# Output projection of a hybrid attention layer: where its weights and outputs wait, which engine adds, and the order of the first up tile's products

## Chip, core, metric

The kernel runs on one core of a Trainium2 chip. The metric is device time in microseconds (us) of one execution. A core has TensorE (PE, matrix products and transposes), VectorE (DVE), ScalarE (ACT), GpSimd (POOL) and SyncE (SP), which here only issues transfers. Each engine works through its own queue in order and waits on semaphores for the others.

## What is computed

One layer over 1024 positions with 1024 features, float32 in and out: two attention head groups, an output projection with a gated residual, then a gated MLP with a causal convolution of width 3.

```python
mixed = jnp.dot(jnp.concatenate([o_mla, o_ca], axis=-1), w_out[l])
x = x + g_a[:, None, :] * mixed

h = modulate(rmsnorm(x, g_mlp_norm[l]), sh_m, sc_m)
u = causal_dwconv(jnp.dot(h, w_up[l]), conv_w[l], conv_b[l])
gate, val = jnp.split(u, 2, axis=-1)
x = x + g_m[:, None, :] * jnp.dot(jax.nn.silu(gate) * val, w_down[l])
```

## The kernel before

Every product is made of three TensorE matmuls on split operands: a high part (a rounded copy, made by `hi_of`) and a low part (the rest, made by `lo_of`); `hi*hi + hi*lo + lo*hi` is summed in PSUM (`gemm3`, `product`). A split is thus one copy on ScalarE and one subtract on GpSimd or VectorE, for each operand tile.

The stages, in the order of the program:

1. Input projections, then attention. Attention handles units (a head and one half of the queries), four row tiles of 128 each. For each row tile the probabilities are split into two 16-bit parts and transposed by a transfer from SP's queue (line 822); `values` multiplies them with v, and after four tiles a unit's output is scaled and written to DRAM, `oT_d` (lines 853 to 859). Input projections of later heads, the up-projections `f_up` and the chunk-attention half of the output projection, `f_oca`, are filled in between. `f_oca` multiplies rows 512 to 1023 of `w_out` and writes the partial sums to DRAM, `part_d`.
2. The output projection's other half (lines 989 to 1055): `load_wo` fetches eight weight pieces of 128x512 through staging tiles and splits them into pages of the pool G4 (8 buffers). Then, for each of eight row tiles t: load the attention output `ol` (256 KB) and split it, load x and the partial sum `pa` (512 KB each), 24 matmuls into PSUM `op`, then three sums, `pa + op`, times the gate `gabc`, plus x; store the result (`x1_d`), take its square sum (ScalarE) and reciprocal root (GpSimd), and scale it in place to `xn2[t]`.
3. Operand pages for the MLP. `mod_T(k, h)` transposes block k of half h (0: tiles 0 to 3, 1: tiles 4 to 7) and applies scale and shift; `bpage` splits. The up projection uses a seven-product scheme of Strassen type in 2x2 blocks: pages b11 and b21 come from half 0, and t3, t1, b22, t2 and t4 are differences of halves, made on VectorE block by block, k = 0 to 3 (lines 1116 to 1127).
4. 22 up tiles, `ff_tile(j)`. `ff_load(j)` fetches two weight tiles `wu` of 512 KB and splits wa and wb; `ff_sums(j)` forms five sums and splits them (wc to wg); `product(..., "t3")` and so on multiply, 12 matmuls each; sums into `c`, convolution, SiLU, product, store.
5. The down projection and the final residual.

The program is written in this order, but a scheduler, working on its own estimates, arranges each engine's queue: a step can be moved ahead of others where its inputs allow, and `tc.issue_after` forces an order. A tile pool with n buffers for a tag lets an instruction that needs a new buffer wait until the oldest one's readers are done; a pool opened in the place of a closed one waits for the tiles that lay there.

Names of buffers in the profile are shortened: `wor` is a staged piece of w_out, `wo` its split page, `ol` and `oh` the attention output's low and high part, `om` a unit's output on its way to `oT_d`, `x`/`x_d` the residual stream and its store, `hv` and `t`/`b` values and pages of stage 3, `p` the PSUM tiles and copies of the up tiles, `PTm`/`hlm` the transposed probabilities and their two parts.

Of the kernel before, what the change touches and what calls it, by code (L numbers as in the profile page):

```python
# [63 lines left out]
def layer_kernel(ctx, tc, I, out):  # L64
# [661 lines left out]
    class Unit:  # L726
# [7 lines left out]
        def scores(u, i):  # L734
# [55 lines left out]
            with tc.high_priority(offset=OFF_P):  # L790
                dve.reciprocal(ri[:], rsum[:, 0:1])
                dve.tensor_scalar(ri[:], ri[:], PSCALE, None, op0=MUL)  # L792
                for x, (p0, p1) in enumerate(pieces):
# [28 lines left out]
                    anchor["sp"] = sp.dma_start_transpose(tt[:, b0:b0 + 2 * w // P, :], hl[:, :2 * w]).ins  # L822
# [4 lines left out]
        def values(u, i):  # L827
# [17 lines left out]
            with tc.high_priority(offset=OFF_V):  # L845
# [7 lines left out]
                if i % 4 == 3:  # L853
                    dst = at.tile([P, 512], F32, name=f"o{u.nm}_{u.g}", tag="o", bufs=1)
# [4 lines left out]
                    sp.dma_start(u.dst_d[r0, u.g * 512:(u.g + 1) * 512], dst[r0])  # L859
# [3 lines left out]
    pair = [0]  # L863
    biases = {}
# [124 lines left out]
    wo = [load_wo(0, n, "a", "v" if n else "p") for n in range(2)]  # L989
    att.__exit__(None, None, None)  # L990
    att_pg.__exit__(None, None, None)
    psA.__exit__(None, None, None)
    G["cm3"].__exit__(None, None, None)
    G["cmv"].__exit__(None, None, None)
# [13 lines left out]
    def mod_T(k, h):  # L1008
# [3 lines left out]
        v = tb.tile([P, 512], F32, name=f"hv2_{k}_{h}", tag="v", bufs=11)  # L1012
# [12 lines left out]
    sp.dma_start(cvp[:], I["pack"][:, C_CV:])  # L1025
    gabc = gb.tile([P, D], F32, name="gabc")
    sp.dma_start(gabc[:], ga_d[:])
    for t in range(NT):
        lo = gb.tile([P, 4, P], F32R, name=f"ol{t}", tag="ol", bufs=3)
        hi = gb.tile([P, 4, P], F32R, name=f"oh{t}", tag="oh", bufs=3)  # L1030
        sp.dma_start(f32(lo[:]), oT_d[0:4, :, t * P:(t + 1) * P].rearrange("k p t -> p k t"))
        hi_of("a", hi[:], f32(lo[:]))
        lo_of("p", lo[:], f32(lo[:]), hi[:])
        x1 = tb.tile([P, D], F32, name=f"x1_{t}", tag="x1", bufs=8)
        sp.dma_start(x1[:], I["x"][t * P:(t + 1) * P, :])
        pa = gb.tile([P, D], F32, name=f"pa{t}", tag="pa", bufs=3)
        sp.dma_start(pa[:], part_d[t])
        pt = ps2.tile([P, 1024], F32, name=f"op{t}", tag="op", bufs=3)
        for n in range(2):
            gemm3(pt[:, n * 512:(n + 1) * 512],  # L1040
                  [(hi[:, k], lo[:, k], wo[n][k][:, 0], wo[n][k][:, 1]) for k in range(4)])
        dve.tensor_tensor(pa[:], pa[:], pt[:], op=ADD)
        dve.tensor_tensor(pa[:], pa[:], gabc[:], op=MUL)
# [6 lines left out]
        if t % 4 == 3:  # L1050
            h = t // 4
            if h == 0:
                for k in range(ND):
                    v0[k] = mod_T(k, 0)
                    bpage("b11" if k < 4 else "b21", k % 4, v0[k], "v" if k % 2 else "p")
# [454 lines left out]
```

## Time and profile before

| | |
|---|---|
| median of three runs | 1411.35 us (1406.68 to 1412.14) |
| the profiled execution | 1412.2 us, its span 1410.4 us |
| TensorE busy | 1237.9 us (88%), mean granted clock 0.928 |
| VectorE busy | 1099.7 us (78%) |
| GpSimd busy | 712.9 us (51%) |
| ScalarE busy | 620.9 us (44%) |
| moved by transfers | 190.57 MB, mean 135 GB/s |

The profile records one execution. Times count from the start of the span. "Busy" sums the durations of an engine's instructions; TensorE's matmuls overlap their neighbours, so a single matmul's duration is longer than the distance to the next. The granted clock is the share of TensorE's full clock that the throttle let through. A row of the timeline names the instruction, what it writes and reads, and in brackets how long its engine sat idle before it and on whom it waited. The prediction shows the lines on which it rests.

### The profile page before, as it was taken

What the parts mean: (1) busy time and instruction counts of PE and PEld (TensorE: products, weight loads), DVE (VectorE), ACT (ScalarE), POOL (GpSimd) and SP (SyncE); (2) the same over time, 40 slices, a digit from 0 to 9 for tenths busy, and PEclk for the clock granted to TensorE, in tenths of its full rate; (3) what the DMA queues carried; (4) which work ended last, traced back from release to release, by engine and by line L of the source; (5) the groups of instructions that cost most, each with busy time, mean ns of one, the idle gap of its engine ahead of it and who ended that gap; (6) DMA issues with size and microseconds to landing.
All of it is one profiled execution on the core that took longest, in us unless ns stands there. A gap on an engine that the chain in (4) does not pass through costs nothing.

```text
span 1410.4 us, 18704 instructions
## 1 busy us (share of the span) xinstructions
PE 1237.9 (88%) x6156; PEld 1012.0 (72%) x6156; DVE 1099.7 (78%) x1861; ACT 620.9 (44%) x1129; POOL 712.9 (51%) x685
## 2 busy tenths in 40 slices
PE   4889798998777689886686999999999999999998
PEld 3788487887656467674565887777778777888886
DVE  6957778675689988873577888988888888788667
ACT  4343445444556545543264444344334443443331
POOL 5454556375555754334563677676667875200000
PEclk9999797999787899996887999999999999999999
DMA  8314558664322667677721323333222223894451
GB/s 313 126 37 83 137 145 185 152 138 106 70 48 46 133 144 170 144 147 222 278 98 45 105 98 127 127 112 128 97 100 87 101 101 117 306 354 128 127 163 60
DMA packets 223689, 190.57 MB, mean 135 GB/s; under 512 B 148708, under 2 KB 166884, under 8 KB 223592
## 3 DMA queue, kind: packets, MB, share of 16 engines
q1 hardware_dynamic: 223592, 189.38, 47.4%
q8 instruction: 48, 0.79, 0.2%
q14 instruction: 49, 0.40, 0.1%
HBM read 117.24 MB, written 37.49 MB: 110 GB/s over the span
## 4 chain that ended last, share of the span: by engine, by line
DVE 21%; PE 17%; POOL 6%; issue 6%; ACT 4%; DMA 2%; SPq 0%; DVEq 0%; POOLq 0%; ACTq 0%
DVE u L1174 5%; DVE u L1173 4%; PE dnA_P L1321 2%; PE dnA_P L1322 2%; PE dnA_P L1323 2%; ACT u L1172 2%; PE dnB_P L1322 1%; PE dnB_P L1321 1%; PE dnB_P L1323 1%; DVE u L1250 1%; DVE c L1245 1%; DVE gmbc L1160 1%; DVE wu L1102 1%; DVE wu L1101 1%; DVE ws L1099 1%
## 5 line engine op out<-in xcount | busy, mean ns | idle before, releaser
L76 ACT ACTIVATE dnP<-dnr 128x1024 fp32r<-128x1024 f32 x73 | 77.3, 1061 | 110.9 <-PE dnA_P L1323 46.4
L1295 DVE TENSOR_TENSOR dnP<-dnr,dnP 128x1024 fp32r<-128x1024 f32 x72 | 90.7, 1264 | 44.4 <-ACT dnP L76 44.2
L1173 DVE SCALAR_TENSOR_TENSOR u<-c,cvp,u 128x1023 f32<-128x1023 f32 x44 | 82.6, 1917 | 47.2 <-ACT u L1172 45.6
L72 POOL TENSOR_SCALAR hlm<-Pm,rim 128x512 f16<-128x512 f32 (+3 forms) x96 | 68.7, 724 | 85.2 <-DVE rim L792 21.6
L1174 DVE SCALAR_TENSOR_TENSOR u<-c,cvp,u 128x1022 f32<-128x1022 f32 x44 | 86.4, 2003 | 0.0
L72 POOL TENSOR_SCALAR hlc<-Pc,ric 128x640 f16<-128x640 f32 (+2 forms) x64 | 46.7, 732 | 72.8 <-DVE ric L792 46.4
L811 DVE SCALAR_TENSOR_TENSOR hlm<-Pm,rim,hlm 128x512 f16<-128x512 f32 (+3 forms) x96 | 67.7, 715 | 8.6 <-POOL hlm L72 8.1
L850 PE MATMUL pvm<-PTm,vt 128*128 128x256 f16 (+1 forms) x320 | 47.0, 295 | 30.3 <-DMA PTm<-hlm 29.7
L789 ACT ACTIVATE Pm<-sm,mm 128x128 f32<-128x128 f32 (+3 forms) x64 | 47.3, 739 | 55.6 <-DVE mm L782 37.5
L850 PEld LDWEIGHTS <-vt 128*128 128x128 f16 x320 | 31.2, 108 | 46.8 <-issue 22.2
L789 ACT ACTIVATE Pc<-sc,mc 128x640 f32<-128x640 f32 (+2 forms) x64 | 42.1, 658 | 46.6 <-DVE mc L778 35.4
L811 DVE SCALAR_TENSOR_TENSOR hlc<-Pc,ric,hlc 128x640 f16<-128x640 f32 (+2 forms) x64 | 50.7, 795 | 14.1 <-POOL hlc L72 13.3
L76 ACT ACTIVATE wc<-ws 128x512 fp32r<-128x512 f32 x22 | 13.9, 633 | 103.0 <-DVE ws L1099 103.0
L1172 ACT ACTIVATE u<-c,cvp 128x1024 f32<-128x1024 f32 x44 | 52.1, 1234 | 14.8 <-DVE c L1245 7.8
L153 PE MATMUL ipq<-wq_s,hT 128*128 128x256 f32 x192 | 57.4, 301 | 1.2 <-ACT wq_s L76 1.2
L154 PE MATMUL ipq<-wq_s,hT 128*128 128x256 f32 x192 | 57.7, 301 | 0.1
L155 PE MATMUL ipq<-wq_s,hT 128*128 128x256 f32 x192 | 57.3, 299 | 0.0
L1249 ACT ACTIVATE u<-u 128x1024 f32<-128x1024 f32 x22 | 23.3, 1061 | 71.1 <-DVE u L1174 71.0
L83 POOL TENSOR_TENSOR wc<-ws,wc 128x512 fp32r<-128x512 f32 x22 | 34.3, 1557 | 36.4 <-ACT wc L76 36.4
L1322 PE MATMUL dnA_P<-dnP 128*128 128x512 f32 x132 | 51.3, 389 | 0.0
L1323 PE MATMUL dnA_P<-dnP 128*128 128x512 f32 x132 | 51.3, 389 | 0.0
L1321 PE MATMUL dnA_P<-dnP 128*128 128x512 f32 x132 | 51.2, 389 | 0.0
(420 smaller groups left out, 4563.0 us busy)
## 6 DMA issues: line engine op xcount, KB each, us to landing
wu<-w_up SPq DMA_DIRECT2D x44, 512.0 KB, 3.5
dnr<-g_d SPq DMA_DIRECT2D x73, 256.0 KB, 4.5
aw<-w_ada SPq DMA_DIRECT2D x48, 256.0 KB, 3.6
g_d<-u SPq DMA_DIRECT2D x22, 512.0 KB, 2.7
dnr<-w_down SPq DMA_DIRECT2D x44, 256.0 KB, 5.4
adaw<-w_ada_a SPq DMA_DIRECT2D x16, 512.0 KB, 6.5
x<-x SPq DMA_DIRECT2D x16, 512.0 KB, 8.7
g_d<-gs SPq DMA_DIRECT2D x22, 256.0 KB, 2.0
```

Source lines behind the costliest of these rows:

```text
L72: pool.tensor_scalar(o, i, s, 1.0, op0=MUL, op1=MUL)
L76: act.activation(o, i, AF.Copy)
L789: act.activation(pr[:, :n], sv, AF.Exp, bias=m[:], scale=-1.0, accum_out=rsum[:, 0:1])
L811: dve.scalar_tensor_tensor(hl[:, w:2 * w], pp, ri[:], hl[:, :w], op0=MUL, op1=SUB)
L850: last = pe.matmul(dst, u.vst(j), mov, start=(x == 0), stop=(x == len(todo) - 1), skip_group_check=True)
L1172: act.activation(u[:], c, AF.Identity, scale=cvp[:, cv + 2:cv + 3], bias=cvp[:, cv + 3:cv + 4])
L1173: dve.scalar_tensor_tensor(u[:, 1:], c[:, :S - 1], cvp[:, cv + 1:cv + 2], u[:, 1:], op0=MUL, op1=ADD)
L1174: dve.scalar_tensor_tensor(u[:, 2:], c[:, :S - 2], cvp[:, cv:cv + 1], u[:, 2:], op0=MUL, op1=ADD)
L1295: r = f(*a, **k)
L1321: pe.matmul(pt, sh, w[:, 0, 0], start=start, stop=False, skip_group_check=add)
L1322: pe.matmul(pt, sh, w[:, 1, 0], start=False, stop=False, skip_group_check=add)
L1323: pe.matmul(pt, sl, w[:, 0, 0], start=False, stop=stop, skip_group_check=add)
```

## The change

The parts, with the names of the diff:

- `load_wo` stages w_out in `atile` (tag A, five buffers, used until then by the adaLN weights) in place of `qtile` (two buffers, shared with attention's squares and copies). This holds for both halves of w_out.
- The last unit's output goes to a `qtile` instead of the single `o` buffer. Its store to `oT_d` is held back and issued behind the first four `ol` loads; the last row tile's transposes are ordered behind the store of the unit before.
- A pool `go` holds `ol` and `oh`, four buffers each instead of three, in the place of the q and k tiles of attention; `o_load` for tiles 0 to 3 stands ahead of the loop, and tile t+4 is loaded after tile t's products. `pa` has four buffers and, with x, is loaded by `x_load`, four tiles ahead too.
- All sums and scalings of stage 2 are on VectorE (some were on GpSimd).
- `ff_load(0)` is issued among the loads, and `ff_sums(0)` after tile 1's sums; the pages `ws` move to a pool that is opened earlier.
- The transposes of half 0 come after tile 4 rather than after tile 3.
- Pages t3 and t2 take the eight buffers of G4, the pool of w_out's pages, instead of new ones.
- Tile 0's five products of stage 3's pages are computed block by block inside the loop that makes the pages, into PSUM of the old stage (`p34`, `p56`, `p7`); its sums into `c0` follow directly. `ff_tile(0)` skips those products and sums.

```diff
     def load_wo(k0, n, he, le):
...
-            raw = qtile(f"wor{k}_{n}")
+            raw = atile(f"wor{k}_{n}")
...
-                        anchor["sp"] = sp.dma_start_transpose(tt[:, b0:b0 + 2 * w // P, :], hl[:, :2 * w]).ins
+                    with tc.issue_after(anchor["om"]) if u is units[-1] and i == 7 else contextlib.nullcontext():
+                        anchor["sp"] = sp.dma_start_transpose(tt[:, b0:b0 + 2 * w // P, :], hl[:, :2 * w]).ins
...
-                    dst = at.tile([P, 512], F32, name=f"o{u.nm}_{u.g}", tag="o", bufs=1)
+                    final = u is units[-1]
+                    dst = qtile(f"o{u.nm}_{u.g}") if final else \
+                        at.tile([P, 512], F32, name=f"o{u.nm}_{u.g}", tag="o", bufs=1)
...
-                    sp.dma_start(u.dst_d[r0, u.g * 512:(u.g + 1) * 512], dst[r0])
+                    if final:
+                        held.append(lambda: sp.dma_start(u.dst_d[r0, u.g * 512:(u.g + 1) * 512], dst[r0]))
+                    else:
+                        anchor["om"] = sp.dma_start(u.dst_d[r0, u.g * 512:(u.g + 1) * 512], dst[r0]).ins
...
+    mlp0 = tc.tile_pool(name="mlp0", bufs=1, side="right", reuse_waits="tile")
+    mp = {"a": mlp0.__enter__()}
+    goo = tc.tile_pool(name="go", bufs=1, side="right", reuse_waits="tile")
+    go = goo.__enter__()
+    def o_load(t):
+        ol[t] = go.tile([P, 4, P], F32R, name=f"ol{t}", tag="ol", bufs=4)
+        oh[t] = go.tile([P, 4, P], F32R, name=f"oh{t}", tag="oh", bufs=4)
+        anchor["ol"] = sp.dma_start(f32(ol[t][:]), oT_d[0:4, :, t * P:(t + 1) * P].rearrange("k p t -> p k t")).ins
+        hi_of("a", oh[t][:], f32(ol[t][:]))
+        lo_of("p", ol[t][:], f32(ol[t][:]), oh[t][:])
+
+    for t in range(4):
+        o_load(t)
+    with tc.issue_after(anchor["ol"]):
+        held[0]()
...
+    sp.dma_start(gabc[:], ga_d[:])
+    for t in range(2):
+        x_load(t)
+    raw0, wa0, wb0 = ff_load(0)
+    for t in range(2, 4):
+        x_load(t)
+    sp.dma_start(cvp[:], I["pack"][:, C_CV:])
     for t in range(NT):
-        lo = gb.tile([P, 4, P], F32R, name=f"ol{t}", tag="ol", bufs=3)
-        hi = gb.tile([P, 4, P], F32R, name=f"oh{t}", tag="oh", bufs=3)
...
+        if t + 4 < NT:
+            o_load(t + 4)
...
-        (dve if t % 2 or t > 5 else pool).tensor_tensor(x1[:], x1[:], pa[:], op=ADD)
+        dve.tensor_tensor(x1[:], x1[:], pa[:], op=ADD)
         sp.dma_start(x1_d[t], x1[:])
         act.activation(pa[:], x1[:], AF.Square, accum_out=ss2[:, t:t + 1])
+        if t + 4 < NT:
+            x_load(t + 4)
...
-        (dve if t > 5 else pool).tensor_scalar(x1[:], x1[:], r2[:, t:t + 1], 1.0, op0=MUL, op1=MUL)
-        if t % 4 == 3:
+        dve.tensor_scalar(x1[:], x1[:], r2[:, t:t + 1], 1.0, op0=MUL, op1=MUL)
+        if t == 1:
+            w0 = ff_sums(0, raw0)
+        if t == 4:
...
+    ready = p34[:], p56[:, :512], p56[:, 512:], p7[:, :512]
     for k in range(4):
...
         bpage("t3", k, t3, "v")
+        product(ready[3], w0[0], "t3", ks=[k])
...
         bpage("t1", k, b12, "v")
+        product(ready[1], w0[2], "t1", ks=[k])
         bpage("b22", k, b22, "v")
+        product(ready[0][:, :512], w0[4], "b22", ks=[k])
...
         bpage("t2", k, b22, "v")
+        product(ready[2], w0[1], "t2", ks=[k])
...
         bpage("t4", k, v0[k + 4], "v")
+        last = product(ready[0][:, 512:], w0[3], "t4", ks=[k])
...
+    dve.tensor_tensor(c0[:, 0], pc[:, :512], pc[:, 512:], op=ADD)
+    dve.tensor_tensor(c0[:, 1], pc[:, :512], ready[2], op=ADD)
+    dve.tensor_tensor(c0[:, 2], c0[:, 1], ready[3], op=ADD)
+    dve.tensor_tensor(c0[:, 1::2], c0[:, 1:3], ready[1].unsqueeze(1).to_broadcast([P, 2, 512]), op=ADD)
+    dve.tensor_tensor(c0[:, 1:3], c0[:, 1:3], ready[0].rearrange("p (a b) -> p a b", a=2), op=ADD)
```

More of the change, by code (lines that the diff above doesn't have):

```diff
@@ L1269, in layer_kernel @@
     gr_gen = gate_row()
[L1270 to L1271 removed]
+    p3_last = [last]
+    cur = w0 + [None, None, c0]
     for j in range(NF):
```

120 lines of the change are left out of this document (60 added, 60 removed).

## The prediction

> **What bounds the kernel now.** I began with the first line of the profile's page, for the execution's own time, and then asked how busy each engine is in stretches cut at the places where the program changes stage. The time around the span is 1412.2 - 1410.4 = 1.8 us, and I make the sum against 1412.2 us, 0.85 us above the median of the three runs (1411.35 us).
>
> ```profile
> span 1410.4 us, 18704 instructions
> ```
> The table by stretches follows; its columns are the stretch, its length, the busy time of TensorE (PE), its weight loads (PEld), VectorE (DVE), ScalarE (ACT) and GpSimd (POOL) with their instructions, the granted TensorE clock, the DMA share and GB/s. The first row lies inside attention, the second is its end, the next three hold the output projection, then come the operand pages (732 to 758), up tile 0's own products (758 to 775) and the other 21 up tiles.
>
> ```profile
> 472.00:503.00 31.00, 18.22 (x91) 13.45 (x89) 27.52 (x71) 15.09 (x31) 26.48 (x23) 0.78 0.76 154
> 640.00:657.00 17.00, 6.15 (x29) 3.89 (x29) 5.47 (x9) 3.90 (x7) 5.45 (x7) 0.50 0.79 190
> 657.00:676.00 19.00, 18.87 (x69) 14.89 (x70) 3.17 (x4) 5.45 (x9) 7.56 (x6) 0.83 0.67 229
> 676.00:690.00 14.00, 2.99 (x9) 1.57 (x7) 10.17 (x7) 5.01 (x9) 7.69 (x4) 0.67 1.04 382
> 690.00:732.00 42.00, 39.35 (x180) 31.62 (x181) 23.14 (x20) 17.55 (x30) 30.82 (x31) 0.95 0.48 178
> 732.00:758.00 26.00, 10.33 (x38) 7.47 (x36) 25.07 (x38) 18.75 (x32) 3.03 (x2) 0.63 0.00 0
> 758.00:775.00 17.00, 16.12 (x63) 12.73 (x64) 9.28 (x11) 5.78 (x11) 11.17 (x8) 0.87 0.29 93
> 775.00:1173.00 398.00, 386.69 (x1668) 312.18 (x1667) 344.82 (x275) 163.29 (x237) 282.67 (x177) 1.00 0.32 108
> ```
> The last row settles how a microsecond counts: the up tiles keep TensorE busy 386.69 of 398 us at clock 1.00, so they are bound by TensorE, and work that reaches them earlier ends earlier by the same amount. From 657 to 775 TensorE is busy only 18.87 + 2.99 + 39.35 + 10.33 + 16.12 = 87.7 of 118 us. The holes are 11 us at 676 to 690 and 15.7 us at 732 to 758. In the second VectorE is busy 25.07 of 26 us, so VectorE bounds that stage and TensorE's work is queued behind it. The first hole is read from the queue on SyncE and from TensorE's own timeline (start, length, engine, line, operation; in brackets the idle time before it and what ended it).
>
> ```profile
> 645.00 0.58 SPq L859 DMA_DIRECT2D oT_d<-om  x1
> ...
> 650.04 0.38 SPq L1031 DMA_DIRECT2D ol<-oT_d  x1
> ...
> 660.98 9.78 SPq L661 DMA_DIRECT2D wor<-w_out  x3
> 670.81 0.42 SPq L1025 DMA_DIRECT2D cvp<-pack  x1
> 674.45 2.25 SPq L1035 DMA_DIRECT2D x<-x  x5
> 676.75 3.14 SPq L1031 DMA_DIRECT2D ol<-oT_d  x3
> ```
> ```profile
> 656.90 0.80 PE L153 MATMUL op<-wo,oh 128*128 128x512 f32 x1 [4.44 <-ACT oh L76]
> ...
> 685.76 0.79 PE L153 MATMUL op<-wo,oh 128*128 128x512 f32 x1 [8.84 <-ACT oh L76]
> ```
> The three last weight loads hold the in-order queue from 660.98 to 670.76, because their two staging buffers are not free; the loads of x (674.45) and of the attention output for tiles 3 to 5 (676.75) stand behind them. TensorE runs out of tiles and waits 8.84 us for tile 3's high part. The end of each stage stands on VectorE's timeline.
>
> ```profile
> 720.64 1.22 DVE L1042 TENSOR_TENSOR pa<-pa,op 128x1024 f32<-128x1024 f32 x1 [1.08 <-PE op L155]
> ...
> 729.77 0.89 DVE L1049 TENSOR_SCALAR x<-x,r 128x1024 f32<-128x1024 f32 x1 [2.38 <-DMA x_d<-x]
> ...
> 732.56 0.69 DVE L1119 TENSOR_TENSOR t<-hv,hv 128x512 f32<-128x512 f32 x1 [1.30 <-ACT hv L1013]
> ...
> 755.64 1.47 DVE L83 TENSOR_TENSOR t<-hv,t 128x512 fp32r<-128x512 f32 x2
> ...
> 775.18 1.22 DVE L1245 TENSOR_TENSOR c<-c,p 128x1024 f32<-128x1024 f32 x1
> ```
> The last projection product ends just before 720.64; the pages run from 732.56 to 755.64 + 1.47 = 757.1; up tile 0's last sum, which waits for its last product, starts at 775.18.
>
> **The change part by part.**
>
> *Start of the projection.* The staging tiles for w_out move from two shared buffers to five free ones, so in the changed order thirteen of sixteen loads stand inside attention and the last three directly behind its last transposes, ahead of the attention-output loads. What is not moved is the dependence: tile 0 needs the output rows written by the transfer issued at 645.00, and its loads stay behind the last transposes, at about 650 as now. On ScalarE tile 0's high part now stands behind the last attention copies and one weight split. I take a start at 656.3 instead of 656.90: a gain of 0.6 us, with bounds of 0 and, if the loads went out right behind the 645.00 write, 5.
>
> *The projection itself.* Eight tiles of 24 matmuls are 192. The chain of waits shows what one costs, second column, at the two clock rates:
>
> ```profile
> 659.05 0.43 PE op L153
> ...
> 664.65 0.23 PE op L153
> ```
> 192 x 0.23 = 44.2 us, which rounded up also carries the eight short transposes that stand among them. After attention's idle end the clock is low: 0.83 granted over 19 us with half rate at first means 19 x 0.17 x 2 = 6.5 us at half rate, which costs 3.2 us. The Trainium skill, in "TensorE: Matmul & The Clock Gate" (Part 1: The HAM clock gate), gives about 3.4 us of sustained work before full rate; by that page the surcharge would be an estimated 1.7 us and the gain of the whole 1.5 us more; this trace does not agree, so the row decides. With 1.5 us of waits for the first low parts the last product ends at 656.3 + 44.2 + 3.2 + 1.5 = 705.2 in place of 720.6: 15.4 us with the start included.
>
> This needs inputs in time. Per tile VectorE now has all four sums:
>
> ```profile
> L1042 DVE TENSOR_TENSOR pa<-pa,op x8: 1215/1222/1224, 676.0 to 720.6; 128x1024 f32<-128x1024 f32 x8
> L1043 DVE TENSOR_TENSOR pa<-pa,gabc x8: 1217/1368/3364, 679.5 to 723.4; 128x1024 f32<-128x1024 f32 x8
> L1046 ACT ACTIVATE pa<-x x8: 1051/1057/1064, 684.0 to 726.8; 128x1024 f32<-128x1024 f32 x8
> L1046 ACT ACTIVATION_READ_ACCUMULATOR pa<-x x8: 184/187/194, 685.0 to 727.8; 128x1 f32 x8
> L1044 DVE TENSOR_TENSOR x<-x,pa x5: 1214/1226/2178, 685.0 to 724.6; 128x1024 f32<-128x1024 f32 x5
> L1044 POOL TENSOR_TENSOR x<-x,pa x3: 2404/3025/3290, 681.0 to 706.7; 128x1024 f32<-128x1024 f32 x3
> ```
> 1.22 + 1.37 + 1.23 and the scale, 0.89 in the row at 729.77, are 4.7 us against 24 x 0.23 = 5.5 us of TensorE: VectorE stays just below. Leaving GpSimd takes 2.4 to 3.3 us of add per tile off its queue, in front of the low-part splits that TensorE waits for. The x loads no longer stand behind the weights; I expect them to be issued near 660 instead of 674.45. Each tile's square on ScalarE (1.06 us) and its mean now stand ahead of the split of the tile four later, on both queues; with x landed by about 668 that split is ready when TensorE comes to it, with x as late as now TensorE waits 674.45 - 660 = 14.5 us less the two tiles (11 us) of lead, so 3.5, and two delayed splits make it 6. Bounds of this part: -2 to +6 around my value. The bytes are not the bound: eight tiles with x, partial sum and store of 0.52 MB each and 0.26 MB of outputs, and 1 MB of up weights, are some 16 MB, in 55 us 290 GB/s; the row at 676 moved 382. Tile 0's seven weight splits on GpSimd lie in that stretch as well, where it was busy 7.56 of 19 us; they cost nothing while it has room, and about 1.3 us each if they delay an output split.
>
> *From the last product to the first page.* 11.9 us now (720.64 to 732.56), a chain of sums, the store of x that must finish before x is scaled in place, transposes and copies. The last x add was one of those lengthened by GpSimd (up to 2178 ns against 1214); that goes: 1.0 us gained, bounds 0 and 2.
>
> *The pages.* The same VectorE instructions in the same number (x38 in their row): 24.5 us as now. The products of tile 0 go between them, five after each block, 60 matmuls of 0.23 = 13.8 us, into a stage where TensorE is busy 10.33 of 26: covered by VectorE's 25 us. If the cover is gone (half rate), 60 x 0.43 = 25.8 us and 10.33 make 36.1, which is 10 us too much. Transposes of blocks 2 and 3 now stand behind waits for earlier blocks' pages on TensorE's in-order queue, with ScalarE's copies and VectorE's differences behind them; there is slack of a block, and I add nothing here, bounds 0 and +10.
>
> *After the pages.* Now 757.1 to 775.18, 18.1 us, for splits of tile 0's weights, 60 products and the wait for the second weight load of tile 1. In the changed order two sums come first (2 x 24.5/38 = 1.3 us), which free the bank of tile 1's first product; this product, done within the pages until now, then takes 12 x 0.23 = 2.8 us. From there both kernels do the same. 18.1 - 4.1 = 14.0 us gained, less 1 us that I allow for tile 1's first splits: 13.0; bounds 10 and 14.
>
> *Attention.* The splits of the first w_out half move out of 472 to 503, where GpSimd was busy 26.48 of 31 us and VectorE 27.52, five of the eight to a place ahead of the second head group's up-projections; five of the second half's go into the last heads. One split costs this:
>
> ```profile
> L76 ACT ACTIVATE wo<-wor x16: 620/630/633, 475.2 to 673.1; 128x512 fp32r<-128x512 f32 x16
> L83 POOL TENSOR_TENSOR wo<-wor,wo x12: 1260/1298/3231, 476.6 to 658.2; 128x512 fp32r<-128x512 f32 x12
> ```
> Eight of them are 8 x 1.30 = 10.4 us of GpSimd; if all of it had been on the path, that would be the gain; moved work can as well delay the place where it lands. I take 0, bounds -10 and +10.
>
> **The sum.** 15.4 + 1.0 + 0 + 13.0 + 0 = 29.4 us. 1412.2 - 29.4 = 1382.8, predicted 1383 us. Its own range is 1376 to 1391.
>
> **The rivals.**
>
> *TensorE becomes the bound of the pages.* For: all rows at 732 to 758 show a clock of 0.63, and short bursts with gaps are what the new order makes. Against: the row at 690, whose end holds the first pages' products with waits and transposes among them, kept 0.95. At half rate the 10 us above: 1383 + 10 = 1393. The Trainium skill, same page (Part 4: PE-mode transpose), says that transposes do not count as work that releases the clock; by that rule the gaps filled with them would stay at half rate. The row at 732 agrees so far as a stretch with mostly transposes stayed low.
>
> *The projection still waits for inputs.* The hole at 676 to 690 stays in another place, because x, the partial sums and the outputs all come through one in-order queue in which each load waits for its buffer. For: 382 GB/s at that hole, with a DMA share above 1, so a burst there can be the limit. Against: four output tiles are asked for before everything else, and the mean need is 290 GB/s. All 14 - 2.99 = 11.0 us back: 1394.
>
> *Attention gains too.* GpSimd's 10.4 us at 472 to 503 were on the path: 1383 - 10 = 1373.
>
> *Slower: SyncE's queue stalls attention.* Thirteen weight loads now stand between the transposes of the attention tiles, each waiting for a split that waits for weight pages of the up-projections. An early-placed load that is not ready stops the transposes behind it, and the value products wait for those. At the longest split (3231 ns) for each, 13 x 3.2 = 42 us: 1383 + 42 = 1425. It decides from 29.4/13 = 2.3 us per load. For: the queue is in order, and 9.78 us were lost that way at 660.98. Against: five buffers instead of two, and in the changed order nearly every load stands after the work it waits for.
>
> **Chances.** Forecast 0.58; pages bound by TensorE 0.14; inputs still late 0.11; attention gains 0.09; slower by the queue 0.08, of which 0.03 with a loss that about cancels the gain. 0.5% is 7 us and about what a measurement of this kernel can tell from no change. Faster 0.92, same 0.03, slower 0.05. The range 1372 to 1398 takes in the bounds of the projection and the pages and leaves out the queue rival and the far ends of the others, some 0.18.
>
> **What would show it.** Right: in the changed profile TensorE has no wait above 3 us between the first output product and the last; that last product ends near 705; x loads are issued near 660; the last page ends near 741, and tile 0's last sum starts within 6 us of it, not 18; GpSimd shows no x add. Wrong: a granted clock near 0.5 with TensorE full during the pages (first rival), TensorE waiting for output splits at 675 to 695 (second), the last attention product ending later than about 656 with SyncE's queue long in w_out loads (slower), or an idle TensorE in the up tiles, which would make the sum worth less than it says.

## The result, and the profile after

The changed kernel took 1390.31 us, median of four runs (1386.21 to 1392.88), beside 1410.82 us of the kernel before in the same session: ratio 0.9857, 95% interval 0.9824 to 0.9890. A second comparison (e8) gave 0.9880 (0.9856 to 0.9904). It is 17 to 20 us faster, where the prediction said 29.4: direction and range held, the size did not.

First the stretches of the profiled execution after (1391.6 us, span 1389.8): busy time of PE, PEld, DVE, ACT and POOL with the number of instructions, then granted clock, DMA share, GB/s. They answer to the rows of the projection and the pages in the prediction.

```profile
657.00:676.00 19.00, 18.65 (x83) 15.09 (x81) 15.48 (x11) 6.11 (x11) 13.26 (x8) 1.00 1.04 402
676.00:690.00 14.00, 8.53 (x29) 6.60 (x30) 8.55 (x8) 4.04 (x9) 11.05 (x12) 0.76 0.80 282
690.00:720.00 30.00, 27.52 (x139) 21.43 (x138) 24.75 (x24) 16.28 (x28) 12.30 (x13) 1.00 0.32 120
719.70:744.10 24.40, 19.43 (x80) 13.65 (x78) 24.21 (x37) 17.22 (x30) 3.50 (x2) 0.93 0.01 5
```

The empty middle of the projection is not gone: from 676 to 690 TensorE works 8.53 of 14 us (2.99 before), and GpSimd is now the fullest of the helpers. Transfers do more in the first row (402 GB/s). In the pages TensorE runs 80 matmuls at 0.93, not 38 at 0.63. The timeline of TensorE shows where it still waits (start, duration, line, what it writes and reads, idle time before and on whom):

```profile
652.13 0.79 PE L154 MATMUL op<-wo,oh 128*128 128x512 f32 x1 [4.53 <-ACT oh L77]
...
682.21 0.80 PE L156 MATMUL op<-wo,ol 128*128 128x512 f32 x1 [4.72 <-POOL ol L84]
...
748.40 0.77 PE L1067 MATMUL p<-b,wa 128*128 128x512 f32 x1 [3.49 <-DVE c L1177]
...
761.14 0.50 PE L1067 MATMUL p<-b,wb 128*128 128x512 f32 x1 [1.39 <-ACT c L1287]
```

And VectorE's timeline has the marks that the prediction used: the sum behind the last projection product, the first page difference, the last page's split, the first tile's last sum.

```profile
706.56 1.22 DVE L1120 TENSOR_TENSOR pa<-pa,op 128x1024 f32<-128x1024 f32 x1 [1.13 <-PE op L156]
...
719.73 0.69 DVE L1156 TENSOR_TENSOR t<-hv,hv 128x512 f32<-128x512 f32 x1 [1.30 <-ACT hv L1039]
...
742.66 1.46 DVE L84 TENSOR_TENSOR t<-hv,t 128x512 fp32r<-128x512 f32 x2
...
748.77 1.22 DVE L1178 TENSOR_TENSOR c<-c,p 128x1024 f32<-128x1024 f32 x1
```

GpSimd's low parts in the projection show what stood ahead of tile 4's (`ol` at 679.95):

```profile
668.15 1.30 POOL L84 TENSOR_TENSOR wd<-wu,wd 128x512 fp32r<-128x512 f32 x1 [2.09 <-DMA ol<-oT_d]
...
673.87 2.28 POOL L84 TENSOR_TENSOR wg<-wu,wg 128x512 fp32r<-128x512 f32 x1
...
679.95 2.20 POOL L84 TENSOR_TENSOR ol<-ol,oh 128x512 fp32r<-128x512 f32 x1
```

One split takes 1.30 us, another 2.28, and so do the two between them: in those microseconds VectorE runs its own sums.

The last sum starts 4.7 us behind the pages (742.66 + 1.46 = 744.1), as forecast, but TensorE's wait at 748.40 hangs on the sum ahead of it, L1177. From these marks, one table for all runs: when the first projection product starts; from there to the last projection sum; on to the first page difference; on to the end of the last page split; on to the end of the span.

| run | starts | projection | to pages | pages | behind | time ratio to before, 95% interval |
|---|---|---|---|---|---|---|
| before | 656.9 | 63.7 | 11.9 | 24.6 | 653.3 | |
| before, once more (e12) | 653.5 | 63.4 | 12.0 | 25.1 | 653.0 | |
| **changed** | 652.1 | 54.4 | 13.2 | 24.4 | 645.7 | 0.9857 (0.9824 to 0.9890) |
| changed, once more (e8) | 647.4 | 54.6 | 13.2 | 24.4 | 645.6 | 0.9880 (0.9856 to 0.9904) |
| e1 staging alone | 654.5 | 57.4 | 11.5 | 24.3 | 653.0 | 0.9965 (0.9949 to 0.9982) |
| e2 products last in the program | 653.7 | 55.3 | 13.2 | 24.3 | 643.8 | 0.9872 (0.9844 to 0.9901) |
| e3 splits late | 643.6 | 47.6 | 17.9 | 25.7 | 644.4 | 0.9853 (0.9828 to 0.9878) |
| e4 other bank | 652.9 | 55.4 | 13.2 | 24.4 | 649.7 | 0.9917 (0.9897 to 0.9938) |
| e5 first tile late | 648.3 | 47.8 | 14.3 | 24.3 | 654.7 | 0.9910 (0.9886 to 0.9934) |
| e6 free bank | 646.5 | 56.5 | 13.2 | 24.4 | 642.6 | 0.9863 (0.9837 to 0.9888) |
| e7 splits on VectorE | 648.8 | 47.7 | 11.6 | 24.6 | 646.6 | 0.9832 (0.9812 to 0.9852) |
| e9 = e6 + e7 | 646.9 | 47.5 | 11.6 | 24.6 | 642.2 | 0.9784 (0.9760 to 0.9807) |
| e10 = e9, all up tiles | 652.7 | 46.9 | 11.6 | 23.6 | 619.2 | 0.9634 (0.9616 to 0.9653) |
| e11 sums back on GpSimd | 651.1 | 56.3 | 14.0 | 24.4 | 645.9 | 0.9890 (0.9858 to 0.9921) |

The forecast in the same form: start 656.3, projection 48.9, 10.9, 24.5, and 640.3 behind (653.3 - 13.0).

### The profile page after: what moved, and what is told of

It is laid out like the page before. It is cut to its first block, busy times and chain, and to the rows that moved or that the text cites. A ratio compares the mean times of both kernels' runs of the same rounds, so it can differ in the third digit from the quotient of the medians.

```text
span 1389.8 us, 18690 instructions
## 1 busy us (share of the span) xinstructions
PE 1233.6 (89%) x6156; PEld 1004.4 (72%) x6156; DVE 1112.7 (80%) x1870; ACT 617.9 (44%) x1129; POOL 694.8 (50%) x676
## 4 chain that ended last, share of the span: by engine, by line
PE 40%; DVE 29%; issue 9%; DMA 7%; ACT 7%; POOL 6%; SPq 1%; DVEq 0%; POOLq 0%; ACTq 0%
DVE u L1222 4%; DVE u L1221 4%; PE dnA_P L1368 2%; PE dnA_P L1370 2%; PE dnA_P L1369 2%; PE p L1069 2%; PE p L1067 2%; PE p L1068 2%; PE sm L764 2%; PE sc L758 2%; PE dnB_P L1370 1%; PE dnB_P L1369 1%; PE dnB_P L1368 1%; ACT u L1220 1%; PE pvm L852 1%
## 5 line engine op out<-in xcount | busy, mean ns | idle before, releaser
L1342 DVE TENSOR_TENSOR dnP<-dnr,dnP 128x1024 fp32r<-128x1024 f32 x72 | 88.2, 1229 | 46.9 <-ACT dnP L77 46.9
L812 DVE SCALAR_TENSOR_TENSOR hlc<-Pc,ric,hlc 128x640 f16<-128x640 f32 (+2 forms) x64 | 53.6, 842 | 10.4 <-POOL hlc L73 10.2
L154 PE MATMUL ipq<-wq_s,hT 128*128 128x256 f32 x192 | 55.5, 292 | 0.9 <-ACT wq_s L77 0.9
L155 PE MATMUL ipq<-wq_s,hT 128*128 128x256 f32 x192 | 55.8, 291 | 0.4 <-POOL wq_s L84 0.3
L156 PE MATMUL ipq<-wq_s,hT 128*128 128x256 f32 x192 | 55.3, 289 | 0.0
```

Of the source, the lines that this page charges most:

```text
L812: dve.scalar_tensor_tensor(hl[:, w:2 * w], pp, ri[:], hl[:, :w], op0=MUL, op1=SUB)
L1342: r = f(*a, **k)
```

## The experiments

### Does one program repeat? (e8 and e12)

> The changed kernel once more, beside the three above. If the attention's end differs between executions of one program by some microseconds, its last projection product and first page difference shift with the attention while the stretches behind keep their lengths: projection 54 to 55 us, last sum to first page difference 13 to 13.5, pages 24 to 24.8. If instead the waits in the projection come and go, these lengths differ by over 2 us.

> The kernel before once more, one look. The changed kernel began its first projection product at 652.13 us in one profile and at 647.37 in another, while every stretch behind kept its length within 0.2 us, so one pair of profiles can't tell whether the attention ended earlier by the change. If the change moved the attention, the kernel before begins its projection at 655 us or later again and keeps 63 to 64.5 us for the projection, 11.9 to the first page difference, 24.5 for the pages and 653.3 behind them. If it was only the executions that differed, it may begin at 647 to 653, with the same four lengths.

The lengths repeat within 0.2 us in the changed kernel and within 0.6 in the one before. (The projection is the loosest: in e2, e4 and e6, which leave it as it is, it took 55.3 to 56.5 us; differences under 2 us are not read from it.) The start does not: 652.1 and 647.4 for one program, and 656.9 and 653.5. So a single pair of profiles says nothing within some 5 us on where attention ends, and the lengths are what the runs below are read by. Attention's own waits repeat, though. These are TensorE's from 600 to 660 us (total, times, longest), before:

```profile
PE pvm L850 <- DMA PTm<-hlm: 12.5, 5, 4.8
PE op L153 <- ACT oh L76: 4.4, 1, 4.4
PE pvm L850 <- DVE om L858: 0.5, 1, 0.5
```
and changed:
```profile
PE pvm L852 <- DMA PTm<-hlm: 5.9, 3, 2.8
PE op L154 <- ACT oh L77: 4.5, 1, 4.5
PE pvm L852 <- DVE om L862: 3.9, 1, 3.9
```

Before: 12.5 + 0.5 us of waits for transposed scores and for the output copy, and 13.4 + 0.5 in the second profile; after: 5.9 + 3.9, and 4.9 + 3.7 in e8. So TensorE has 3 to 5 us less of these waits at attention's end, whichever execution is taken. That alone doesn't make the projection start 3 to 5 us earlier. An estimate of the start comes from the measured times, which rest on several executions: they fell by 20.2 us in the first comparison and by 16.9 in the second, each with some 3 to 5 us to either side, and the four lengths of the table fell by 15.8 (753.5 before, the mean of its two rows, and 737.7). That leaves 4.4 and 1.1 us for the start.

### Staging alone (e1)

```diff
 def load_wo(k0, n, he, le):          # in the kernel before
-            raw = qtile(f"wor{k}_{n}")
+            raw = atile(f"wor{k}_{n}")
```

> The kernel before with one part of the change: w_out's rows are staged in the attention's tiles (atile) instead of qtile; nothing else. Theory: this alone changes the order in which SyncE issues the last score transposes, and so explains why in the changed kernel the last values matmul ended at 647.6 us instead of 652.5 and the first projection product began at 652.13 instead of 656.90. Then the store of the last but one unit is issued near 640 (645.00 before) and the time falls by 2 to 5 us, to 1406 to 1409. Rival 1: the attention's gain came from holding back the last unit's store and from the tile loads that stand ahead of it; then the store stays near 645 and the time within 1 us of before. Rival 2 (the prediction's slower case): the 13 early w_out loads stand in front of transposes; then attention ends later than 652.5 and the time is above 1412.

Measured: 0.9965, some 5 us faster, and the same waits inside attention as in the changed kernel:

```profile
PE op L153 <- ACT oh L76: 7.1, 1, 7.1
PE pvm L850 <- DMA PTm<-hlm: 5.1, 3, 2.2
PE pvm L850 <- DVE om L858: 3.7, 1, 3.7
```

So the staging tiles alone shorten these waits. What SyncE did there stands in its queue, before:

```profile
632.02 0.46 SPq L859 DMA_DIRECT2D oT_d<-om  x1
632.58 0.54 SPq L661 DMA_DIRECT2D wor<-w_out  x1
635.91 0.32 SPq L681 DMA_DIRECT2D part_d<-co  x1
636.34 8.61 SPq L822 DMA_TRANSPOSE PTm<-hlm  x6
```
and changed:
```profile
633.67 0.46 SPq L866 DMA_DIRECT2D oT_d<-om  x1
634.22 5.86 SPq L824 DMA_TRANSPOSE PTm<-hlm  x4
640.18 0.54 SPq L866 DMA_DIRECT2D oT_d<-om  x1
```

Before, a w_out load and a store of the other half's partial sum stood in front of the last eight transposes, and the queue stood still from 633.1 to 635.9; after, no load stands there. The store of the last but one unit went out at 643.30 in e1, not near 640, and the first projection product waits 7.1 us for the high part instead of 4.4. The projection fell from 63.7 to 57.4, as w_out's second half no longer arrives in the middle of it. All four lengths together fell by some 7 us (753.5 to 746.2), more than the 5 us by which the time fell. So the time lies where the theory put it, but for another reason: the gain is in the projection, and nothing of it is left for an earlier start.

Where attention's gain goes is seen from the sixteen stores of its outputs on SyncE's queue (`oT_d<-om`), the start of the first and then the distances in us:

| run | first store | to the fourth | to the fourteenth | to the first projection product |
|---|---|---|---|---|
| before | 438.69 | 72.7 | 120.6 | 24.9 |
| before, once more (e12) | 434.61 | 72.7 | 121.4 | 24.8 |
| e1 staging alone | 446.74 | 64.2 | 123.1 | 20.4 |
| changed | 444.14 | 65.1 | 124.4 | 18.5 |
| changed, once more (e8) | 445.92 | 62.7 | 121.3 | 17.5 |

The stretch that five of the eight splits of w_out's first half have left is 8 to 10 us shorter, and the first store, ahead of which GpSimd now makes these five (424 to 433 us in the changed kernel), is 5 to 12 us later. The staging alone does both; that it is these splits which delay the first store is likely, but not shown. At the end, staging gives 4.4 of the 6 to 7 us, and the rest of the change 2 to 3; which part of it (the held store, the order of the last transposes, the early tile loads) was not tried alone. The slower rival, w_out loads that stop the transposes, was not seen at attention's end.

### The first tile's products behind the pages (e2), and its whole part (e5)

In e2 only the place of the calls changes:

```diff
 for k in range(4):
-        product(ready[3], w0[0], "t3", ks=[k])
 ...
+    product(ready[3], w0[0], "t3")
+    product(ready[2], w0[1], "t2")
 ...
```

> The changed kernel with one part undone: the first up tile's five products run whole behind the page loop instead of block by block inside it; the sums follow as in the changed kernel. The prediction gave this part 13.0 us. Theory now: TensorE is the bound behind the pages, so what counts is TensorE's work and waits there. Undone, 60 products (14.4 us at 0.24, some 2 more while the clock is low) come behind the pages, but the 3.5 us wait ahead of the second tile's first product and its 2.6 us at the low clock go: 9 to 12 us slower than the changed kernel, 1399 to 1403, with the pages still 24 to 25 us long. Rival 1: the full 13 to 15 us, 1403 to 1406. Rival 2: the products inside the pages lengthen the pages, so taking them out shortens the stretch from the first page difference to the last page split below 23 us, and the loss is under 8 us.

None of the three: 0.9872, behind the pages 643.8. The scheduler moved only a part. Of the 60 matmuls 33 still ran inside the pages, the first two microseconds behind the first page difference, though their calls stand behind the loop. The other 27 (`we`, `wg` and three of `wf`) ran behind the pages' end at 746.5, ahead of the second tile:

```profile
724.37 0.50 PE L1067 MATMUL p<-t,wc 128*128 128x512 f32 x1 [1.50 <-ACT t L77]
...
746.62 0.39 PE L1067 MATMUL p<-t,we 128*128 128x512 f32 x1
...
753.58 0.47 PE L1067 MATMUL p<-b,wa 128*128 128x512 f32 x1 [0.66 <-DVE c L1177]
```

These 27 cost next to nothing there. The second tile's wa product is done 9.9 us behind the pages in e2 and 9.5 in the changed kernel, which spends the time on the 3.49 us of wait and on 5.25 us for wa's 12 matmuls at the low clock (2.8 in e2). What lets the 33 run inside is that the weights are split already. So e5 takes that away, with the split tiles in the pool that opens behind the pages, as before:

```diff
-    mp["a" if tag in ("raw", "w2", "ws") else "b"]
+    mp["a" if tag in ("raw", "w2") else "b"]
 ...
-        if t == 1:
-            w0 = ff_sums(0, raw0)
 ...
+    w0 = ff_sums(0, raw0)            # behind the page loop
+    product(ready[3], w0[0], "t3")
 ...
```

> The changed kernel with the whole of its part on the first up tile undone: its weight sums and splits wait for tiles that are free only behind the page loop, as in the kernel before, so its five products follow there too. (Moving the products alone in the program moved nothing: they still ran between the pages, and the time stayed at 1390.) Theory: the part earned some 7.6 us behind the pages (measured from the last page split to the end: 653.3 us before, 645.7 after) and cost 4.7 us of wait for tile 4's low part in the projection plus 1 to 3 us of VectorE's time up to the first page difference. Undone: projection 47 to 50 us long instead of 54.4, first page difference 5 to 8 us earlier relative to the first projection product, 8 to 14 us lost behind the pages; net 1 to 8 us slower than the changed kernel. Rival 1 (the prediction's sum): 13 us slower, as it costs nothing in the projection. Rival 2: what it costs ahead of the pages outweighs what it earns: faster than the changed kernel by over 1 us.

Measured: 0.9910 against 0.9880, some 4 us slower than the changed kernel. By the table, 9.0 us are lost behind the pages (654.7), 6.7 us are won in the projection (47.8 instead of 54.4 to 54.6), and 1.1 lost between. The theory holds, and so does the forecast's length of the projection (48.9), once the splits are out of it; its start at half rate lasts 6.2 us here (648.27 to 654.50), where 6.5 were forecast. The only wait of TensorE left in the projection of e5 is the one ahead of its first product (4.4 us).

What the 33 matmuls inside the pages are worth with the splits left early was not tried; for the other 27, e2 shows no gain.

### The splits on GpSimd's queue (e3)

```diff
-        if t == 1:
+        if t == 5:
             w0 = ff_sums(0, raw0)
```

> The changed kernel with the first up tile's weight sums and splits placed behind output tile 5 in the program instead of behind tile 1; on GpSimd's queue the five low parts wc to wg then stand behind tile 7's reciprocal root instead of ahead of tile 4's low part. Theory: tile 4's products waited 4.72 us for a low part (GpSimd, 679.95 to 682.15) that stood behind those five splits (663.8 to 676.1). Then the wait goes under 1.5 us, the last projection sum starts 3 to 5 us earlier (701 to 704 instead of 706.56), and the end comes 1 to 5 us earlier, less what the splits cost beside the pages: 1385 to 1390. Rival 1: tile 4 waited for its own load and its high part (ScalarE 676.09, itself behind tile 1's square); then the wait stays above 3 us and the time at 1390. Rival 2: the splits, now 712 to 726, make the first page products wait and press VectorE: the gain is taken back, 1390 to 1394.

The wait for tile 4's low part is gone and the projection takes 47.6 us. So GpSimd's queue was the cause, not the load or ScalarE. But the time can't be told from the changed kernel's (0.9853): from the last sum to the first page difference it took 17.9 us instead of 13.2, and the pages 25.7 instead of 24.4. VectorE there, in e3:

```profile
697.52 1.75 DVE L84 TENSOR_TENSOR b<-hv,b 128x512 fp32r<-128x512 f32 x1
...
709.05 1.77 DVE L1156 TENSOR_TENSOR t<-hv,hv 128x512 f32<-128x512 f32 x1
710.86 0.69 DVE L1159 TENSOR_TENSOR hv<-hv,hv 128x512 f32<-128x512 f32 x1
```

A 128x512 operation takes 0.69 us at 710.86; of the eight from 697.52 to 709.05 the six beside GpSimd's low parts take 1.75 to 1.77. Of the 6.8 us that the queue had cost, 6.0 came back as slower VectorE, which is rival 2's mechanism. All four lengths together are 2.1 us shorter than the changed kernel's; the median, 1385.95 us, lies in the theory's range, and a gain of that size can't be told from none.

### The two engines beside each other (e7)

```diff
-        lo_of("p", w[:, 1], src, w[:, 0])
+        lo_of(le, w[:, 1], src, w[:, 0])     # "v" for up tile 0
 ...
-    bpage(..., k % 4, v0[k], "v" if k % 2 else "p")
+    bpage(..., k % 4, v0[k], "v")
```

> The changed kernel with the first up tile's seven low parts and the four of the first half's pages that GpSimd made given to VectorE. Theory: a 128x512 low part takes 0.69 us on VectorE and 1.29 on GpSimd, where it runs alone; where both run two-input operations, GpSimd's took 2.28 and VectorE's 1024-column ones 2.2 to 2.3 instead of 1.22. So VectorE loses about as much by GpSimd's work as by doing it (11 x 0.69 = 7.6 us against some 8 us of stretched operations from 660 to 719), GpSimd's queue is free for tile 4's low part, and that wait (4.72 us) goes: the 1024-column sums take 1.22 to 1.3 us, projection 48 to 50 us instead of 54.4, the last sum to the first page difference 10 to 11.5 us instead of 13.2; 5 to 8 us faster than the changed kernel. Rival 1: the stretch comes from DMA writing into the same memory, not from GpSimd: the operations stay at 2.2 us, VectorE gets 7.6 us more work and becomes the projection's bound; within 1 us or slower. Rival 2: only the wait goes, the chain behind it is unchanged or longer, as VectorE's queue now holds all splits: 2 to 4 us faster.

Measured: 0.9832, 6 to 7 us faster than e8 in the same session; projection 47.7, 11.6 to the pages. VectorE does 11 more splits and is no later. Its three sums per output tile, in the changed kernel (shortest/median/longest in ns):

```profile
L1120 DVE TENSOR_TENSOR pa<-pa,op x8: 1207/1220/1222, 660.3 to 706.6; 128x1024 f32<-128x1024 f32 x8
...
L1121 DVE TENSOR_TENSOR pa<-pa,gabc x8: 1210/1224/2315, 662.6 to 707.8; 128x1024 f32<-128x1024 f32 x8
...
L1122 DVE TENSOR_TENSOR x<-x,pa x8: 1212/1226/2196, 669.2 to 711.8; 128x1024 f32<-128x1024 f32 x8
```
and the product of the tile (L1121 above) in e7:
```profile
L1122 DVE TENSOR_TENSOR pa<-pa,gabc x8: 1211/1216/1598, 661.2 to 698.2; 128x1024 f32<-128x1024 f32 x8
```

With GpSimd's splits beside them, products and residual sums take up to 2.3 us; without, 1.22; the exceptions (1.60 at 681.68, 1.71 at 675.87) fall beside low parts of the output tiles, which GpSimd still makes. The first sum, L1120, which reads one operand from PSUM, is never stretched, not even at 660.27 with the transfers at 402 GB/s and GpSimd splitting; that speaks against transfers as the cause, rival 1. e7 settles it: with the transfers as busy (397 GB/s) and GpSimd almost idle, the products and residual sums from 655 to 671 us all take 1.22 us.

```profile
655.00:671.00 16.00, 16.00 (x73) 13.21 (x72) 12.74 (x16) 5.66 (x10) 2.80 (x1) 1.00 1.04 397
```

The Trainium skill says why in "SBUF — State Buffer" (Who interferes with whom): a VectorE instruction with two SBUF inputs and a GpSimd instruction that reads SBUF need the same read port, and one blocks until the other is done; a VectorE instruction with at most one SBUF input, outside its 2-port modes, does not contend. The rows agree: 1.22 for L1120 always, and some 1.1 us on top of the others. They also agree with the Trainium skill's "GPSIMD Engine Reference" (8. Key points), by which VectorE is about twice as fast at elementwise work: 0.69 and 1.29 us for a low part.

### Where the second up tile starts (e4, e6)

```diff
+    q1_1 = bank("p1", "p1_1")        # e4: first of its pool
 ...
+            if not j:
+                bank("G", "p_gx")    # e6: so p1_1 falls on bank 6
+            cp = act.activation(d[:, 3], q1[:], AF.Copy).ins
+        with contextlib.nullcontext() if j else tc.issue_after(cp):
             ug, uv = conv(cg, j), conv(cv, NF + j)
```

> The changed kernel with one allocation moved: the second up tile's first accumulator takes the first PSUM banks of its pool (those of the transposes, free when the last page's transpose has been read) instead of the bank that the first tile's fourth sum frees. Theory: the 3.49 us in which TensorE waited for that sum at 744.9 to 748.4, and the 2.6 us that the 12 products wa then took longer at the low clock, are what is missing from the 13.0 us that the prediction gave the part behind the pages; with the bank free the 12 products run inside the page stretch: 3 to 7 us faster than the changed kernel, 1383 to 1387, and the stretch of pages stays 24 to 25 us. Rival 1: the 12 products in the page stretch delay page products and so the pages' end: within 1.5 us of the changed kernel. Rival 2: TensorE only waits later, for the second tile's low parts (GpSimd until 757): under 2 us of gain and a new wait of over 3 us on GpSimd between 745 and 760.

e4 missed: slower than the changed kernel, 0.9917. The bank was not one of the transposes' but another one of the first tile's, and the first tile's convolution then stood in front of the accumulator's copy on ScalarE. TensorE in e4:

```profile
762.78 0.79 PE L1067 MATMUL p<-b,wb 128*128 128x512 f32 x1 [5.89 <-ACT c L1289]
```

> The changed kernel with two things moved: the second up tile's first accumulator gets bank 6, which the last but one page's transposes leave (in the run before it got bank 0, which the first tile's third sum frees, and waited 1.66 us for that), and the first tile's convolution is placed behind that accumulator's copy on ScalarE (the copy waited behind it, and TensorE 5.89 us for the copy). Theory: TensorE goes from the last page's products straight to the second tile's wa: the 3.49 and 1.39 us waits fall under 0.5 us each, the 12 wa products take 2.9 to 3.6 us instead of 5.46, and the end comes 5 to 8 us earlier than in the changed kernel. Rival: TensorE then waits for the second tile's wc to wg (ScalarE and GpSimd, 746 to 757), or the convolution of tile 0 comes late and holds back the tiles behind it: a new wait over 3 us between 745 and 800, gain under 3 us.

In e6 TensorE goes on 0.6 us behind the pages, and at full clock (0.40 us for a matmul, not 0.77):

```profile
741.14 0.40 PE L1067 MATMUL p<-b,wa 128*128 128x512 f32 x1
```

It reaches the third tile's first product 18.0 us behind the pages (758.49), the changed kernel 25.1 (769.21): 7.1 us earlier. But from the pages' end to the span's end only 3.1 us are left (642.6 against 645.7), and the ratio, 0.9863, can't be told from the changed kernel's. Theory and rival are each right in a part: the two waits are gone (0.7 us for a sum and 1.6 for low parts of GpSimd stand there instead), and the up tiles behind take back 4 us. They are not bound by TensorE alone.

### Both, and all up tiles (e9, e10)

> The two edits of the runs with the splits on VectorE and with bank 6 together. Theory: they act at different places (ahead of the pages; behind them), so the gains add up to stage lengths of 47.5 to 48 us for the projection, 11.5 to 12 from the last sum to the first page difference, 24.5 for the pages and 642 to 644 from there to the end, against 54.5, 13.2, 24.4 and 645.7 in the changed kernel: 9 to 11 us faster than it, 1377 to 1381 beside 1388. Rival: VectorE bounds the first up tiles, so that starting TensorE earlier only makes it wait there: behind the pages 645 to 647 as with the splits on VectorE alone, 7 us faster than the changed kernel, 1382 to 1384.

e9: 1375.26 us, 0.9784; the lengths are those of e7 ahead of the pages and of e6 behind them, so the gains add. In e10 the low parts of all 22 up tiles are made on VectorE as well (`le = "v"` everywhere).

> The same, and the weight splits of all 22 up tiles on VectorE instead of GpSimd. In the changed kernel an up tile takes 20.06 us on average from the second to the last, where TensorE's 84 products of 0.2267 us need 19.04; VectorE's two convolution sums of 1024 columns take 1.9 to 2.1 us each and GpSimd's low parts 1.6 to 2.1. Theory (the two engines slow each other wherever both run two-input operations): 7 low parts cost VectorE 4.8 us a tile and free it of about as much, tiles fall to 19.04 to 19.5 us and the end comes 10 to 20 us earlier than with both edits alone. Rival 1: the convolution sums are that long alone; then VectorE has 4.8 us more in each tile, over 20 us of work, and the kernel becomes 20 to 60 us slower. Rival 2: the tile's 20.06 us come from waits for copies on ScalarE, not from VectorE or GpSimd; within 3 us.

1355.57 us, 0.9634 of the kernel before: the fastest of all, and 19.7 us faster than e9, as the theory said. The wa products of the up tiles, in the changed kernel and in e10 (starts of the first and the last matmul):

```profile
L1067 PE MATMUL p<-b,wa x84: 389/389/767, 748.4 to 1152.4; 128*128 128x512 f32 x84
```
```profile
L1067 PE MATMUL p<-b,wa x84: 389/389/389, 735.4 to 1118.6; 128*128 128x512 f32 x84
```

A product has four matmuls on this line, the last 2.0 us behind the first. So (1152.4 - 2.0 - 748.4) / 20 = 20.1 us a tile stand against (1118.6 - 2.0 - 735.4) / 20 = 19.1, next to TensorE's own 7 x 2.72 = 19.04 (twelve products take 2.72 us, as from 769.21 to 771.93 in the changed kernel). VectorE's convolution sums from 800 to 1130 (us in all, mean ns), changed and e10:

```profile
L1222 DVE SCALAR_TENSOR_TENSOR u<-c,cvp,u 128x1022 f32<-128x1022 f32 x34 | 68.9, 2065 | 0.0
L1221 DVE SCALAR_TENSOR_TENSOR u<-c,cvp,u 128x1023 f32<-128x1023 f32 x33 | 63.3, 1956 | 35.0 <-ACT u L1220 35.0
```
```profile
L1223 DVE SCALAR_TENSOR_TENSOR u<-c,cvp,u 128x1022 f32<-128x1022 f32 x36 | 45.0, 1278 | 0.0
L1222 DVE SCALAR_TENSOR_TENSOR u<-c,cvp,u 128x1023 f32<-128x1023 f32 x36 | 44.6, 1280 | 7.0 <-ACT u L1221 7.0
```

They are 0.68 and 0.79 us shorter without GpSimd's splits. TensorE's longest waits in the changed kernel, from 800 to 1130 us (total, times, longest):

```profile
PE p L1067 <- ACT c L1287: 5.9, 7, 1.0
PE p L1069 <- POOL wc L84: 3.4, 7, 0.9
```

With two shorter ones they make 11.5 us; in e10 TensorE has none and is busy 330.00 of 330 us. Whether VectorE's longer sums or GpSimd's late low parts hold it up was not separated: e10 removes both. This is not part of the change, but it is the likely taker of e6's 4 us.

### The sums back on GpSimd (e11)

```diff
-        dve.tensor_tensor(x1[:], x1[:], pa[:], op=ADD)
+        (dve if t % 2 or t > 5 else pool).tensor_tensor(x1[:], x1[:], pa[:], op=ADD)
 ...
+        (dve if t > 5 else pool).tensor_scalar(x1[:], x1[:], r2[:, t:t + 1], ...)
```

> The changed kernel with one part undone: the residual sums of output tiles 0, 2 and 4 and the scaling of tiles 0 to 5 go back from VectorE to GpSimd, as in the kernel before. The prediction gave this move nothing on the path ahead of the last product. Theory: GpSimd's queue, already behind with the first up tile's splits, gets 3 sums and 6 scalings of 1024 columns more, each beside VectorE's operations: tile 4's low part and the later ones come later still, projection 56 to 66 us instead of 54.5, 2 to 10 us slower than the changed kernel. Rival: the splits stand ahead of all of them in GpSimd's queue and VectorE has that much less to do, so the projection stays 54 to 55 us and the time within 1.5 us.

Undecided. The wait for tile 4's low part grew from 4.7 to 5.8 us and the way to the pages from 13.2 to 14.0, but the projection's 56.3 us lies within what e2, e4 and e6 showed without this edit, and the ratio's interval, 0.9858 to 0.9921, holds theory and rival.

## Why the prediction was right in sign and too large

- **Attention and start: 0.6 forecast, 1 to 4 us by the estimate above.** The rival put 10 us on GpSimd at 472 to 503 us. The stretch around it is 8 to 10 us shorter, but attention's first store comes 5 to 12 later, which fits the prediction's reason for its 0, that "moved work can as well delay the place where it lands". The 6 to 7 us at attention's end, which the prediction did not have, come from SyncE's queue behind 632, 4.4 of them by the staging (e1). The 4.8 us by which the first pair of profiles differ at the start are in part chance.
- **Projection: 48.9 us forecast, 54.4 measured.** The step that failed is the sentence on tile 0's seven splits on GpSimd, that they "cost nothing while it has room". The prediction had the price beside it, "about 1.3 us each if they delay an output split", and set it to nothing. GpSimd had no room: beside VectorE a split took up to 2.28 us, not 1.3, GpSimd was busy 13.26 and 11.05 us of the two windows of 19 and 14, and tile 4's low part came late; TensorE waited 4.72 us and went on at a low clock (0.76 from 676 to 690). Without the splits (e5) it takes 47.8, with them on VectorE (e7) 47.7. The second rival named the right place, "waiting for output splits at 675 to 695", and the wrong cause, the queue of loads; x was issued from 658.92 on, as forecast. What the moved sums themselves are worth stayed undecided (e11).
- **To the pages: +1.0 forecast, -1.3 measured.** GpSimd still makes four page splits there, beside VectorE; with them on VectorE it is 11.6 (e7), while e5, which only takes the weight splits away, has 14.3.
- **Pages: 24.5 forecast, 24.4 measured.** VectorE sets them, the 60 products were covered, and the first rival (half rate) did not occur: 0.93 granted, 80 matmuls.
- **Behind the pages: 13.0 forecast, 7.6 measured.** Two steps failed. The forecast let two sums free the second tile's bank; it takes four, as its tile holds two accumulators and the fourth sum reads the other: 4.3 us from the pages to the product instead of 1.3, and a cold clock, and a copy that stood behind the convolution. And "from there both kernels do the same" counted TensorE alone: e6 had the forecast's time at the third tile (18.0 us; 4.1 + 1 and five products of 2.72 make 18.7) and still kept 10.7 us, not 13.0, and e10 shows that VectorE and GpSimd beside each other hold the tiles up as well.

Net, the part on the first up tile earned 9.0 us behind the pages and 1.1 ahead of them, and cost 6.7 in the projection (e5), 3.4 us in place of 13.0: its free cover was the mis-sized term. The terms add up by construction: 4.8 (start, first pair) + 9.3 - 1.3 + 0.2 + 7.6 = 20.6, the difference of the two spans. Open: why e1's first product waits 7.1 us for its high part, and how much of the start's spread belongs to the throttle.

## What to carry to other kernels

Before work is called hidden on an idle engine, look at what runs beside it: on GpSimd a split is not only slow, it lengthens operations of VectorE next to it that read two operands from SBUF (1.22 us became up to 2.3), and giving it to the busier engine was faster. Work that leaves a full stretch is looked for again where it lands. A gain behind a stage is read at the next point where the bound engine itself stands, and the accumulator's bank is freed by the last reader of its whole tile. And where a scheduler orders the queues, undo a part by its resource (a tile, a bank), not by moving its lines.

## Not expected of the hardware

Eleven profiles of the changed kernel and its variants, with the same work ahead of the projection: its first product started between 643.6 (e3, mean granted clock 0.92 in the first 620 us) and 653.7 us (e2, 0.90), while every length behind repeated within 0.2 us when the changed kernel was run twice. And two engines that each finish alone in 0.69 and 1.29 us take 1.75 and up to 2.28 beside each other.
